# State-space stage of a hybrid backbone block: first weights split earlier, more projections at the opening, transfers by channel block

## The chip, the cores and the metric

The kernel runs on one core of one Trainium2 chip. The metric is the device time of one execution in microseconds (us); lower is better. Engines are named as in the profile: PE (TensorE matmul), PEld (its weight loads), DVE (VectorE), ACT (ScalarE), POOL (GpSimd) and SP (the queue that issues all DMA transfers here). Each engine runs its own instructions in the order in which they stand; semaphores join the engines.

## The reference

One layer over 1024 latent tokens and 256 context tokens of width 1024. The change touches the second of the two token mixers, an S5 state-space model: 512 channels in 32 groups of 16, with 64 complex states a group, run forward and backward.

```python
hl = modulate(rmsnorm(xl, norm1_w[l]), mod_l[0], mod_l[1])
hc = modulate(rmsnorm(xc, norm1_w[l]), mod_c[0], mod_c[1])
pl = jnp.split(hl @ w_in[l], split_idx, axis=-1)
pc = jnp.split(hc @ w_in[l], split_idx, axis=-1)
...
lam_bar, b_bar = s5_discretize(a_re[r], a_im[r], log_step[r], b_re[r], b_im[r])
xs_ctx = s5_scan(flip_if(gc, rev, 1), lam_bar, b_bar, x0)
xs_lat = s5_scan(flip_if(gl, rev, 1), lam_bar, b_bar, xs_ctx[:, -1])
y_lat = y_lat + flip_if(s5_readout(cr, ci, xs_lat), rev, 1)
...
mix_l = (jax.nn.sigmoid(pl[7]) * ya_l + jax.nn.sigmoid(pl[8]) * yb_l) @ w_o[l]
```

`pl[6]` is the S5 input u; `pl[7]` and `pl[8]` are the gates of the merge. The other mixer (gated delta rule) and the MLP with a 3x3 convolution follow and are not touched.

## The kernel before, in words

**Start.** `startup` normalises and transposes the tokens. `modulate` (lines 176 to 200) makes the activations in two parts whose sum is exact enough for float32: ACT rounds a high half (`hl_hi`, `hc_hi`, line 191), DVE recomputes the exact value (line 192), and DVE and POOL by turns subtract to get the low half (`hl_lo`, `hc_lo`, line 194), k block by k block: first latent tokens 0 to 511, then 512 to 1023, then the context.

**The stream of projections.** `gemm_stream` (lines 432 to 478) is a generator. Its 20 jobs are 128 columns of `w_in` each: four for u (units of 512, 512 and 256 tokens), eight for one gate and two for the other (two units of 512), six more with one unit. A job's weights are loaded (`w_raw`, line 442, two buffers), cast to a high half by ACT (`w_hi`, line 447) and subtracted to a low half by POOL (`w_lo`, line 448); the split of the next job's weights and the load of the one after that are issued at the start of a job. Per k block there are three matmuls (high by high, high weights by low activations, low weights by high activations; line 465), and the generator yields after each one:

```python
yield width / 512 * 0.232
```

After a unit, ACT copies it out of PSUM (`gth`, lines 473 and 477) and SP stores it: u to the scratch `u_d` (line 475), gates to `g_d` (line 478).

**The S5 stage.** `s5_stage` works on eight blocks of four groups, h = 0 to 7 ("a group" in the text is one such block of four). For each: `tables` (DVE, lines 484 to 488, products for the g and h tables), `twiddle` (DVE, the same lines on 768 columns), `decays` (ACT), `load` (SP, `s5u` from `u_d`), `weights` (POOL `s5dd`, PE `g_ps`, `ez_ps` and `e_ps`, ACT copies), `toeplitz` (a small DVE sum at line 603, then eight SP copies `s5tm`, line 606), `inputs` (PE `s_ps`, line 618), `rotate` (DVE, lines 629 to 631), `scan` (DVE, lines 637 and 639), `states` (DVE, lines 649 to 652), `outputs` (PE `y_ps`, line 663, ACT Gelu, SP store to `y_d`). Block h+1 is prepared inside block h.

Between these steps `fill(us)` pulls matmuls out of the stream until their booked costs use up the given microseconds, so the order of the program sets how many projection matmuls PE finds between two S5 steps. The whole stage stands under `tc.manual_schedule()`, which keeps each engine's order as written; after it, a scheduler with a model of its own orders instructions. Ahead of the first `fill`, `s5_stage` writes sums for complex products on POOL (`triples`, lines 517 to 523) and three memsets (lines 525 to 527).

Of the kernel before, what the change touches and what calls it, by code (L numbers as in the profile page):

```python
# [61 lines left out]
class Kernel:  # L62
# [188 lines left out]
    def s5_setup(self, sp, tmp):  # L251
        nc, ins, ps = self.nc, self.ins, self.ps
        v = nc.vector
        G = 32
        car = tmp.tile([32, 2, 2, 64], F32, name="car")
        nc.sync.dma_start(car[:, 0], ins["s5_a_re"].rearrange("o r g n -> g (o r) n"))
        nc.sync.dma_start(car[:, 1], ins["s5_a_im"].rearrange("o r g n -> g (o r) n"))
        st = tmp.tile([128, G], F32, name="st")
        for r in range(2):
            nc.sync.dma_start(st[r * 64:(r + 1) * 64, :], ins["s5_log_step"][0, r:r + 1, :].to_broadcast([64, G]))  # L260
        ap = ps.tile([128, 512], F32, tag="dl", name="a_ps")
        for i in range(2):
            self.transpose(ap[:, i * G:(i + 1) * G], car[:, i].rearrange("g r n -> g (r n)"))
        a = tmp.tile([128, 2, G], F32, name="a")
        v.tensor_copy(a, ap[:, :2 * G].rearrange("p (i g) -> p i g", g=G))

# [223 lines left out]
    def s5_stage(self, p, u_d, y_d, stream):  # L490
        nc, ps = self.nc, self.ps
# [9 lines left out]
        def tile(n):  # L501
            return firsts[n].pop() if firsts[n] else new(n)
# [4 lines left out]
        tt = p.tile([128, 2, 768], F32, name="s5tt")  # L507
        tv = tt.rearrange("p c (g m) -> p c g m", g=4)
        t4 = p.tile([128, 4, 768], F32, name="s5t")
        G = 32  # L510
        triples = []
        for name, x, y, n, conj in (("g", self.s5_pg, bb, 8, False), ("h", self.s5_ph, cc, 8, True),
# [12 lines left out]
        g_.memset(b2, 0.0)  # L525
        g_.memset(zo[0:64, :, 0:2], 0.0)
        g_.memset(zo[64:128, :, 768:770], 0.0)
        st = {}
        spent = [0.0]

        def fill(us):
            spent[0] -= us
            while spent[0] < 0:
                c = next(stream, None)
                if c is None:
                    spent[0] = 0.0
                    return
                spent[0] += c

        def gs(h):  # L540
            return slice(4 * h, 4 * h + 4)

        def tables(h):
            hh = p.tile([128, 2, 4, 8, 16], F32, name="s5h", bufs=2)
            gg = p.tile([128, 2, 4, 8, 16], F32, tag="s5r", name="s5g", bufs=2)
            t = [t4[:, i, :512].rearrange("p (g i q) -> p g i q", g=4, i=8) for i in (2, 3)]
            for out, (x, y) in zip((gg, hh), triples):
                xs = [a[:, gs(h), :, None].to_broadcast([128, 4, 8, 16]) for a in x]
                ys = [a[:, gs(h), None, :].to_broadcast([128, 4, 8, 16]) for a in y]
                self.outer3(out[:, 0], out[:, 1], xs, ys, t)  # L550
            st[h] = {"hh": hh, "gg": gg}

        def twiddle(h):
            t3 = tt.rearrange("p c (g a b) -> p c g a b", g=4, a=12)
            t = [t4[:, i].rearrange("p (g a b) -> p g a b", g=4, a=12) for i in (2, 3)]
            xs = [a[:, gs(h), :, None].to_broadcast([128, 4, 12, 16]) for a in triples[2][0]]
            ys = [a[:, gs(h), None, :].to_broadcast([128, 4, 12, 16]) for a in triples[2][1]]
            self.outer3(t3[:, 0], t3[:, 1], xs, ys, t)

        def decays(h):  # L560
            for k in range(4):
                nc.scalar.mul(rho[:, k], self.s5_msk, self.s5_rho[:, 4 * h + k:4 * h + k + 1])

        def load(h):
            u = tile("u")
            r0 = h % 2 * 64
            for j in range(8):
                nc.sync.dma_start(u[j * 16:(j + 1) * 16, :, 0:160],
                                  u_d[h // 2][j, r0:r0 + 64, :].rearrange("(g q) c -> q g c", q=16))
            st[h]["u"] = u  # L570

        def weights(h):
            hh, gg = st[h]["hh"], st[h]["gg"]
            gt = tile("gt")
            dd = p.tile([16, 4, 16], F32, name="s5dd")
            g_.tensor_tensor(dd, self.s5_d[:, gs(h), None].to_broadcast([16, 4, 16]),
                             self.ident[0:16, None, 0:16].to_broadcast([16, 4, 16]), op=OP.mult)
            nc.scalar.copy(b2[0:64, :, :, 0:16], bb[0:64, :, gs(h), :])
            nc.scalar.copy(b2[64:128, :, :, 32:48], bb[64:128, :, gs(h), :])
            for i in range(2):  # L580
                tp = ps.tile([128, 4, 128], F32, tag="tp", name="g_ps")
                for k in range(4):
                    self.transpose(tp[:, k, :], gg[:, i, k].rearrange("p j q -> p (j q)"))
                nc.scalar.copy(gt[:, i], tp)
            e_sb = p.tile([16, 4, 240], F32, tag="s5r", name="s5e", bufs=2)
            ez = ps.tile([128, 4, 16], F32, tag="tp", name="ez_ps")
            for k in range(4):
                for i in range(2):
                    nc.tensor.matmul(ez[0:16, k, :], lhsT=bb[:, i, 4 * h + k, :], rhs=cc[:, i, 4 * h + k, :],
                                     start=(i == 0), stop=(i == 1))  # L590
            fill(1.2)
            ed = ps.tile([128, 4, 128], F32, tag="tp", name="e_ps")
            for k in range(4):
                for i in range(2):
                    nc.tensor.matmul(ed[0:48, k, :], lhsT=b2[:, i, k, :], rhs=hh[:, i, k].rearrange("p i q -> p (i q)"),
                                     start=(i == 0), stop=(i == 1))
            nc.scalar.copy(e_sb[:, :, 0:112], ed[32:48, :, 16:128])
            nc.scalar.copy(e_sb[:, :, 128:240], ed[0:16, :, 0:112])
            st[h].update(gt=gt, e=e_sb, ez=ez, dd=dd)

        def toeplitz(h):
            e_sb = st[h]["e"]
            v.tensor_add(e_sb[:, :, 112:128], st[h]["ez"][0:16], st[h]["dd"])
            tm = tile("tm")
            for j in range(8):
                nc.sync.dma_start(tm[j * 16:(j + 1) * 16], e_sb[:, :, (7 - j) * 16:(7 - j) * 16 + 128])
            st[h]["tm"] = tm
# [15 lines left out]
        def rotate(h):  # L623
            q = t4.rearrange("p c (g m) -> p c g m", g=4)
            for k in range(2):
                ks = slice(2 * k, 2 * k + 2)
                for i in range(2):
                    s = st[h]["s"][2 * k + i][:, None].to_broadcast([128, 2, 2, 192])
                    v.tensor_mul(q[:, 2 * i:2 * i + 2, ks], s, tv[:, :, ks] if i == 0 else tv[:, ::-1, ks])
            v.tensor_sub(t4[:, 0], t4[:, 0], t4[:, 2])  # L630
            v.tensor_add(t4[:, 1], t4[:, 1], t4[:, 3])
# [23 lines left out]
        def outputs(h):  # L655
            s = st.pop(h)
            u, tm, x, hh = s["u"], s["tm"], s["x"], s["hh"]
            yp = ps.tile([128, 4, 128], F32, tag="tp", name="y_ps")
            for k in range(4):
                pairs = ((tm[:, k, :], u[:, k, 32:160]), (hh[:, 0, k].rearrange("p i q -> p (i q)"), x[:, 0, k, :]),  # L660
                         (hh[:, 1, k].rearrange("p i q -> p (i q)"), x[:, 1, k, :]))
                for n, (l, r) in enumerate(pairs):
                    nc.tensor.matmul(yp[:, k, :], lhsT=l, rhs=r, start=(n == 0), stop=(n == 2))
            yo = tile("y")
            nc.scalar.activation(yo, yp, AF.Gelu_apprx_tanh)
            r0 = h % 2 * 64
            for i in range(8):
                nc.sync.dma_start(y_d[h // 2][r0:r0 + 64, i, :].rearrange("(g q) c -> q g c", q=16),
                                  yo[i * 16:(i + 1) * 16])

        fill(14.1)
        tables(0)
        fill(8.0)
        weights(0)
        load(0)
        toeplitz(0)
        twiddle(0)
        decays(0)
        fill(6.0)
        inputs(0)  # L680
        for h in range(8):
            nxt = h + 1 < 8
            rotate(h)
            fill(4.0)
            if h:
                outputs(h - 1)
            if nxt:
                tables(h + 1)
                load(h + 1)
                fill(8.0)  # L690
                weights(h + 1)
            scan(h)
            if nxt:
                toeplitz(h + 1)
            states(h)
            if nxt:
                fill(6.0)
                inputs(h + 1)
                twiddle(h + 1)
                decays(h + 1)  # L700
                fill(3.0)
        fill(1e9)
        outputs(7)

    def late_gates(self, d, g7_d, banks, tags):
# [1012 lines left out]
```

## Time and profile before

| | us |
|---|---|
| median of 3 runs | 1945.08 (1944.63 to 1948.92) |
| profiled execution | 1944.63 |
| its span, first to last instruction | 1942.9 |
| PE busy | 1817.5 (94%) |
| DVE busy | 1342.3 (69%) |
| POOL busy | 818.1 (42%) |
| ACT busy | 722.7 (37%) |
| mean granted PE clock | 0.967 |

The S5 stage with its stream lies between about 63 and 384 us of the span. Busy shares are means over stages with different limits, so for one stage they must be taken from that stage's stretch of the time line. A PE that reads as busy is not always at its peak, since overlapping matmuls are counted whole; the distance between the starts of two matmuls says how fast it goes. The granted clock is 1.0 at 2.4 GHz and 0.5 at 1.2 GHz.

### The profile page before, as it was taken

To read this page: it belongs to the slowest core of one execution; us is meant where nothing else is said; L and a number is where in the kernel's file an instruction comes from. 1 tells how busy PE (TensorE), PEld (TensorE's weight loads), DVE (VectorE), ACT (ScalarE), POOL (GpSimd) and SP (SyncE) were. 2 spreads that over 40 slices of the span, in tenths; PEclk is the share of its full clock that TensorE was granted. 3 is DMA by queue.
4 is the path that set the end of the run, shared out by engine and by line. 5 is a ranking of instruction groups with operands and counts; after the bars stand their busy time and mean duration, and the time that the engine had idled before them with its cause. 6 is when DMAs were issued, how large, how long until landed. Compare 5 with 4: busy or idle time off the path is not lost.

```text
span 1942.9 us, 27849 instructions
## 1 busy us (share of the span) xinstructions
PE 1817.5 (94%) x10922; PEld 1502.9 (77%) x10922; DVE 1342.3 (69%) x1932; ACT 722.7 (37%) x1457; POOL 818.1 (42%) x552
## 2 busy tenths in 40 slices
PE   8289999899999997898899999999999999999997
PEld 3178888777799986787778887788888888888886
DVE  7849999667756546767645334887777777767778
ACT  5513232345444656677642233322212221221222
POOL 1521332346536156545522342444434434442543
PEclk9689999999999998999999999999999999999999
DMA  8033343444412400000344422211111111111102
GB/s 310 24 78 77 90 111 84 130 147 136 136 54 71 129 23 1 2 2 13 125 156 132 129 83 77 65 55 44 44 54 44 54 44 51 47 44 44 55 22 87
DMA packets 190517, 149.30 MB, mean 77 GB/s; under 512 B 25647, under 2 KB 163888, under 8 KB 190386
## 3 DMA queue, kind: packets, MB, share of 16 engines
q1 hardware_dynamic: 190386, 147.52, 25.5%
q8 instruction: 86, 1.41, 0.3%
q14 instruction: 45, 0.37, 0.1%
HBM read 125.99 MB, written 19.40 MB: 75 GB/s over the span
## 4 chain that ended last, share of the span: by engine, by line
PE 58%; DVE 3%; ACT 3%; issue 1%; POOL 1%; DMA 0%; POOLq 0%; SPq 0%; DVEq 0%; ACTq 0%
PE up_ps L227 24%; PE dn_ps L1473 12%; PE pw L227 5%; PE pab L227 4%; PE gl L227 2%; PE pg L227 2%; PE dps L1101 1%; PE ty_ps L1149 1%; PE o_ps L1183 1%; PE ds_ps L1155 1%; PE dps L961 1%; PE ks_ps L1142 1%; ACT Pe L1028 1%; PE pz L227 1%; PE o_ps L1174 1%
## 5 line engine op out<-in xcount | busy, mean ns | idle before, releaser
L1464 DVE SCALAR_TENSOR_TENSOR cacc<-up_ps,colC,cacc 128x945 f32<-128x945 f32 (+3 forms) x360 | 430.3, 1197 | 59.0 <-ACT cacc L1454 51.7
L219 POOL TENSOR_TENSOR w_lo<-w_raw,w_hi 128x1024 fp32r<-128x1024 f32 (+1 forms) x100 | 219.2, 2192 | 417.5 <-ACT w_hi L218 417.1
L227 PE MATMUL up_ps<-h_lo,w_hi 128*128 128x512 f32 x704 | 278.4, 395 | 0.0
L227 PE MATMUL up_ps<-h_hi,w_hi 128*128 128x512 f32 x704 | 277.8, 396 | 0.5 <-DVE cacc L1464 0.5
L227 PE MATMUL up_ps<-h_hi,w_lo 128*128 128x512 f32 x704 | 278.2, 395 | 0.0
L218 ACT CAST w_hi<-w_raw 128x1024 fp32r<-128x1024 f32 (+1 forms) x110 | 105.2, 957 | 371.0 <-PE up_ps L227 163.8
L1483 DVE TENSOR_TENSOR x<-dn_ps,x 128x512 f32<-128x512 f32 x160 | 109.6, 687 | 114.1 <-PE dn_ps L1473 113.0
L227 PEld LDWEIGHTS up_ps<-h_hi,w_hi 128*128 128x128 f32 x704 | 132.3, 188 | 31.9 <-issue 0.9
L227 PEld LDWEIGHTS up_ps<-h_hi,w_lo 128*128 128x128 f32 x704 | 132.6, 188 | 31.0
L227 PEld LDWEIGHTS up_ps<-h_lo,w_hi 128*128 128x128 f32 x704 | 132.5, 188 | 30.9
L448 POOL TENSOR_TENSOR w_lo<-w_raw,w_hi 128x1024 fp32r<-128x1024 f32 x20 | 69.3, 3468 | 195.5 <-ACT w_hi L447 195.4
L465 PE MATMUL pj<-hl_hi,w_lo 128*128 128x512 f32 x272 | 108.7, 400 | 38.4 <-POOL w_lo L448 38.4
L1473 PE MATMUL dn_ps<-wd_lo,g_hi 128*128 128x512 f32 x352 | 138.1, 392 | 0.0
L1473 PE MATMUL dn_ps<-wd_hi,g_lo 128*128 128x512 f32 x352 | 137.5, 391 | 0.0
L1473 PE MATMUL dn_ps<-wd_hi,g_hi 128*128 128x512 f32 x352 | 135.5, 392 | 0.1
L465 PE MATMUL pj<-hl_hi,w_hi 128*128 128x512 f32 x272 | 108.2, 398 | 1.3 <-ACT hl_hi L191 1.3
L465 PE MATMUL pj<-hl_lo,w_hi 128*128 128x512 f32 x272 | 108.7, 400 | 0.8 <-DVE hl_lo L194 0.8
L1287 POOL TENSOR_TENSOR g_lo<-cacc,g_hi 128x1024 fp32r<-128x1024 f32 (+1 forms) x23 | 53.4, 2323 | 92.4 <-ACT g_hi L1286 89.0
L465 PEld LDWEIGHTS pj<-hl_hi,w_lo 128*128 128x128 f32 x272 | 51.8, 190 | 50.2 <-POOL w_lo L448 38.9
L227 PE MATMUL pj<-hl_hi,w_hi 128*128 128x512 f32 (+1 forms) x256 | 90.0, 351 | 0.0
L227 PE MATMUL pj<-hl_hi,w_lo 128*128 128x512 f32 (+1 forms) x256 | 88.9, 347 | 0.0
L227 PE MATMUL pj<-hl_lo,w_hi 128*128 128x512 f32 (+1 forms) x256 | 88.7, 346 | 0.0
(535 smaller groups left out, 4387.3 us busy)
## 6 DMA issues: line engine op xcount, KB each, us to landing
w_raw<-in_w_in SPq DMA_DIRECT2D x46, 512.0 KB, 4.7
w_raw<-in_w_up SPq DMA_DIRECT2D x44, 512.0 KB, 3.8
ada_w<-in_w_ada SPq DMA_DIRECT2D x64, 256.0 KB, 2.7
wd_raw<-in_w_down SPq DMA_DIRECT2D x22, 512.0 KB, 3.6
wa<-in_w_ada SPq DMA_DIRECT2D x16, 512.0 KB, 6.3
g_d<-gth SPq DMA_DIRECT2D x32, 256.0 KB, 2.0
t<-g_d SPq DMA_DIRECT2D x32, 256.0 KB, 3.8
w_raw<-in_w_o SPq DMA_DIRECT2D x16, 512.0 KB, 4.1
```

Source lines behind the costliest of these rows:

```text
L218: self.rounded = nc.scalar.copy(hi[:, :kt, :m], raw[:, :kt, :m]).ins
L219: self.lowered = (eng or nc.gpsimd).tensor_sub(lo[:, :kt, :m], raw[:, :kt, :m], r32(hi[:, :kt, :m])).ins
L227: nc.tensor.matmul(out, lhsT=w[a][:, k, :m], rhs=h[b][k][:, sl] if isinstance(h[b], list) else h[b][:, k, sl], start=(n == 0), stop=(n == ...
L448: nc.gpsimd.tensor_sub(w[1], raw, r32(w[0]))
L465: nc.tensor.matmul(ps[:, :width], lhsT=w[a][:, k], rhs=h[b][:, k, :width], start=(e == 0), stop=(e == 3 * KT - 1))
L961: nc.tensor.matmul(kp[:, h, :], lhsT=self.kT[c][:, h, :], rhs=self.kT[c][:, h, :], start=True, stop=True)
L1028: nc.scalar.copy(pe[g, :, g], pp[g])
L1101: nc.tensor.matmul(o, lhsT=l, rhs=x, start=start, stop=stop, skip_group_check=True)
L1287: (eng or self.nc.gpsimd).tensor_sub(pair[1][sl], x, r32(pair[0][sl]))
L1464: tap[:] = [v.scalar_tensor_tensor(out=o, in0=ui[:, r0 + dy:r1 + dy, c0 + dx:c1 + dx], scalar=cw[:, t * NFT + ct:t * NFT + ct + 1], in1=o, ...
L1473: nc.tensor.matmul(out, lhsT=g[a][:, i * 128:(i + 1) * 128], rhs=w[b][:, h * 512:(h + 1) * 512], start=(first and n == 0), stop=(last and ...
L1483: v.tensor_add(x2, dn, x2)
```

## The change

1. `fill` is defined ahead of the POOL sums, and `fill(0.5)` is called there. The first call of the generator loads and splits the weights of jobs 0 and 1 and issues three matmuls.
2. The opening: 14.1 and 8.0 booked ahead of `weights(0)` become 0.5, 30.0 and 12.0; `twiddle(0)`, `decays(0)` and `load(0)` stand ahead of `weights(0)`, and 6.0 ahead of `inputs(0)` becomes 4.0.
3. In the loop 8.0, 6.0 and 3.0 become 7.0, 5.0 and 2.5. What is left of the stream after block 7 is pulled by `fill(1e9)` as before.
4. `load` and the store in `outputs`: four transfers with all 128 partitions, one for each of the four groups of a block, in place of eight with 16 partitions.

```diff
+        st = {}
+        spent = [0.0]
+
+        def fill(us):
...
+        fill(0.5)
         G = 32
         triples = []
...
             u = tile("u")
             r0 = h % 2 * 64
-            for j in range(8):
-                nc.sync.dma_start(u[j * 16:(j + 1) * 16, :, 0:160],
-                                  u_d[h // 2][j, r0:r0 + 64, :].rearrange("(g q) c -> q g c", q=16))
+            for g in range(4):
+                nc.sync.dma_start(u[:, g, 0:160], u_d[h // 2][:, r0 + 16 * g:r0 + 16 * g + 16, :])
...
-            r0 = h % 2 * 64
-            for i in range(8):
-                nc.sync.dma_start(y_d[h // 2][r0:r0 + 64, i, :].rearrange("(g q) c -> q g c", q=16),
-                                  yo[i * 16:(i + 1) * 16])
-
-        fill(14.1)
+            for g in range(4):
+                r0 = h % 2 * 64 + 16 * g
+                nc.sync.dma_start(y_d[h // 2][r0:r0 + 16].rearrange("q i c -> i q c"), yo[:, g])
+
+        fill(30.0)
         tables(0)
-        fill(8.0)
-        weights(0)
-        load(0)
-        toeplitz(0)
         twiddle(0)
         decays(0)
-        fill(6.0)
+        load(0)
+        fill(12.0)
+        weights(0)
+        toeplitz(0)
+        fill(4.0)
         inputs(0)
...
                 tables(h + 1)
                 load(h + 1)
-                fill(8.0)
+                fill(7.0)
                 weights(h + 1)
...
-                fill(6.0)
+                fill(5.0)
                 inputs(h + 1)
                 twiddle(h + 1)
                 decays(h + 1)
-                fill(3.0)
+                fill(2.5)
```

How the change moves instructions, at three places (rows of the program's order; a name ahead of the arrow is what is written).

POOL from the end of `startup` to the S5 sums, before:

```order
L90 TENSOR_TENSOR rs<-rst,mhalf 128x1
L194 TENSOR_TENSOR hl_lo<-xnT,hl_hi 128x512 x8
L194 TENSOR_TENSOR hc_lo<-xnT,hc_hi 128x256 x4
L521 TENSOR_TENSOR s5dg<-s_pg 128x256
...
L527 MEMSET s5zo 64x2x2
L448 TENSOR_TENSOR w_lo<-w_raw,w_hi 128x1024 x3
```

and with the change:

```order
L90 TENSOR_TENSOR rs<-rst,mhalf 128x1
L448 TENSOR_TENSOR w_lo<-w_raw,w_hi 128x1024 x2
L194 TENSOR_TENSOR hl_lo<-xnT,hl_hi 128x512 x8
L194 TENSOR_TENSOR hc_lo<-xnT,hc_hi 128x256 x4
L534 TENSOR_TENSOR s5dg<-s_pg 128x256
...
L540 MEMSET s5zo 64x2x2
L448 TENSOR_TENSOR w_lo<-w_raw,w_hi 128x1024 x3
```

The low halves of jobs 0 and 1 now stand ahead of the activations' low halves; those of job 2 and later still stand behind the S5 sums.

DVE at the opening, in block 0 (the difference; lines 484 to 488 on 768 columns are `twiddle`, 603 is `toeplitz`, 629 is `rotate`):

```order
 L488 TENSOR_TENSOR s5h<-s5h,s5t 128x512
-L603 TENSOR_TENSOR s5e<-ez_ps,s5dd 16x4x16
 L484 TENSOR_TENSOR s5t<-s_w,s5sw 128x768
...
 L488 TENSOR_TENSOR s5tt<-s5tt,s5t 128x768
+L603 TENSOR_TENSOR s5e<-ez_ps,s5dd 16x4x16
 L629 TENSOR_TENSOR s5t<-s_ps,s5tt 128x2x384 x4
```

The twiddle products no longer stand behind the sum that needs PE's `ez_ps`.

SP around the store of block 5 and the load of block 7, before:

```order
L606 DMA s5tm<-s5e 16x4x128 x8
L478 DMA g_d<-gth 128x512
L442 DMA w_raw<-in_w_in 128x8x128
L478 DMA g_d<-gth 128x512
L668 DMA y_d<-s5y 16x4x128 x8
L568 DMA s5u<-u_d 16x4x160 x8
L478 DMA g_d<-gth 128x512
L442 DMA w_raw<-in_w_in 128x8x128
```

and with the change:

```order
L606 DMA s5tm<-s5e 16x4x128 x8
L478 DMA g_d<-gth 128x512 x2
L442 DMA w_raw<-in_w_in 128x8x128
L668 DMA y_d<-s5y 8x16x128 x4
L569 DMA s5u<-u_d 128x1x160 x4
L478 DMA g_d<-gth 128x512
L442 DMA w_raw<-in_w_in 128x8x128
L606 DMA s5tm<-s5e 16x4x128 x8
```

Two eight-fold issues became four-fold, and one store of a gate moved ahead of the weight load.

## Rows read from the trace of the kernel before

**Rows 1.** Stretches: busy us (count) of PE, PEld, DVE, ACT, POOL; clock, DMA share, GB/s.
```profile
60.00:80.00 20.00, 3.02 (x22) 1.78 (x20) 18.39 (x27) 15.78 (x25) 10.30 (x7) 0.60 0.00 0
80.00:100.00 20.00, 0.00 (x0) 0.00 (x0) 16.58 (x22) 0.00 (x0) 17.04 (x16) 0.50 0.00 0
240.00:260.00 20.00, 20.00 (x118) 16.83 (x117) 19.39 (x20) 6.62 (x15) 9.62 (x3) 1.00 0.46 109
```
**Rows 2.** Time line of the opening: start, duration, engine, line, operation, count, [idle before <-releaser].
```profile
57.52 1.99 ACT L447 CAST w_hi<-w_raw 128x1024 fp32r<-128x1024 f32 x2
63.37 0.55 DVE L192 TENSOR_SCALAR xnT<-xnT,am,modc 128x512 f32<-128x512 f32 x1 [0.88 <-ACT hl_hi L191]
65.23 1.45 POOL L194 TENSOR_TENSOR hl_lo<-xnT,hl_hi 128x512 fp32r<-128x512 f32 x1 [8.71 <-DVE xnT L192]
...
88.02 0.41 DVE L194 TENSOR_TENSOR hc_lo<-xnT,hc_hi 128x256 fp32r<-128x256 f32 x1
101.12 5.50 POOL L448 TENSOR_TENSOR w_lo<-w_raw,w_hi 128x1024 fp32r<-128x1024 f32 x2
103.90 0.79 PE L465 MATMUL pj<-hl_hi,w_lo 128*128 128x512 f32 x1 [38.41 <-POOL w_lo L448]
119.74 0.37 ACT L473 COPY gth<-pj 128x256 f32<-128x256 f32 x1 [2.33 <-PE pj L465]
```
**Rows 3.** Time line of PE: projection matmuls, and s_ps of two following groups.
```profile
108.33 0.48 PE L465 MATMUL pj<-hl_hi,w_hi 128*128 128x512 f32 x1
109.58 0.40 PE L465 MATMUL pj<-hl_hi,w_lo 128*128 128x512 f32 x1
115.72 0.39 PE L465 MATMUL pj<-hl_hi,w_lo 128*128 128x512 f32 x1
...
225.81 2.77 PE L618 MATMUL s_ps<-s5u,s5gt 128*128 128x192 f32 x16
256.67 2.77 PE L618 MATMUL s_ps<-s5u,s5gt 128*128 128x192 f32 x16
```
**Rows 4.** Time line of DVE in the groups, and of GpSimd's weight subtractions.
```profile
133.29 0.94 DVE L488 TENSOR_TENSOR s5tt<-s5tt,s5t 128x768 f32<-128x768 f32 x1
138.61 2.36 POOL L448 TENSOR_TENSOR w_lo<-w_raw,w_hi 128x1024 fp32r<-128x1024 f32 x1 [14.84 <-ACT w_hi L447]
139.74 3.55 DVE L629 TENSOR_TENSOR s5t<-s_ps,s5tt 128x768 f32<-128x768 f32 x4 [5.51 <-PE s_ps L618]
207.29 0.69 DVE L486 TENSOR_TENSOR s5h<-s5dh,s_c 128x512 f32<-128x512 f32 x1 [0.43 <-PE y_ps L663]
226.66 3.55 DVE L629 TENSOR_TENSOR s5t<-s_ps,s5tt 128x768 f32<-128x768 f32 x4 [0.52 <-PE s_ps L618]
238.15 0.69 DVE L486 TENSOR_TENSOR s5h<-s5dh,s_c 128x512 f32<-128x512 f32 x1 [1.73 <-PE y_ps L663]
240.25 3.58 POOL L448 TENSOR_TENSOR w_lo<-w_raw,w_hi 128x1024 fp32r<-128x1024 f32 x1 [11.88 <-ACT w_hi L447]
241.65 3.73 DVE L639 TENSOR_TENSOR_SCAN s5zo<-s5rho,s5t 64x736 f32<-64x736 f32 x1
247.11 1.69 DVE L639 TENSOR_TENSOR_SCAN s5zo<-s5rho,s5t 64x736 f32<-64x736 f32 x1
```
**Rows 5.** Time line of PE and DVE in the last group.
```profile
346.18 3.65 PE L595 MATMUL e_ps<-s5h,s5b 128*48 128x128 f32 x16 [5.03 <-ACT s5gt L584]
357.14 3.55 DVE L629 TENSOR_TENSOR s5t<-s_ps,s5tt 128x768 f32<-128x768 f32 x4 [0.71 <-PE s_ps L618]
380.79 1.09 PE L663 MATMUL y_ps<-s5x,s5h 128*128 128x128 f32 x4 [0.59 <-DVE s5x L651]
```
**Rows 6.** Time line of the SP queue, and the cast that waited for a weight load.
```profile
331.10 3.60 SPq L668 DMA_DIRECT2D y_d<-s5y  x8
334.80 3.65 SPq L568 DMA_DIRECT2D s5u<-u_d  x8
343.97 1.04 ACT L447 CAST w_hi<-w_raw 128x1024 fp32r<-128x1024 f32 x1 [6.91 <-DMA w_raw<-in_w_in]
```

More of the change, by code (lines that the diff above doesn't have):

```diff
@@ L509, in s5_stage @@
         t4 = p.tile([128, 4, 768], F32, name="s5t")
+        st = {}
+        spent = [0.0]
+        def fill(us):
+            spent[0] -= us
+            while spent[0] < 0:
+                c = next(stream, None)
+                if c is None:
+                    spent[0] = 0.0
+                    return
+                spent[0] += c
+        fill(0.5)
         G = 32
@@ L527, in s5_stage @@
         g_.memset(zo[64:128, :, 768:770], 0.0)
[L528 to L538, printed above, removed]
         def gs(h):
```

## The prediction

> **What bounds the kernel now.** Read the granted clock and the chain first: one core, and the chain that ended last is mostly TensorE from the query projections on. The change sits earlier, in the state-space (S5) stage, so the question is what ends last there and whether a gain in it is carried to the end. The table by stretches comes next [rows 1]: from 60 to 100 us TensorE has 3 us of work in 40, while VectorE is busy for 35 of them and GpSimd for 27; by 240 to 260 us TensorE is full and VectorE has 19.4 of 20. So there are two regimes: an opening in which TensorE starves, and a steady stage in which TensorE and VectorE are nearly balanced.
>
> The time line of the opening tells why it starves [rows 2]. The two high halves of the first projection weights are cast on ScalarE at 57.5. The first matmul that needs a low half waits 38.41 us, until 103.90, for GpSimd's subtraction at line 448, which starts only at 101.12 although GpSimd had idled 8.71 us ahead of 65.23: it is written behind the low halves of the activations and the S5 sums. The first projection's last copy-out starts at 119.74.
>
> In the steady stage one group of S5 lasts 30.86 us by its s_ps starts [rows 3]. A full-rate 512-column matmul starts every (115.72 - 109.58) / 27 = 0.2274 us [rows 3], where the code books 0.232, so booked time counts 0.98. The group's bookings, 4 + 8 + 1.2 + 6 + 3 = 22.2, are 21.8 us; the remaining 9.0 are S5's own matmuls. VectorE needs three group starts from 139.74 to 226.66, 86.92 us, less the two waits shown, 0.43 and 0.52 [rows 4]: 28.66 a group of its own work. That is with about one operation a group held up: the scan at 241.65 takes 3.73 beside a GpSimd weight subtraction, its twin at 247.11 takes 1.69.
>
> **The change, part by part.** *Weights first.* The pair of low halves now precedes the activations' low halves on GpSimd, where the time line has a gap. TensorE then takes the first projection at the pace at which activations appear; the last one on VectorE ends at 88.43 [rows 2], and the last three half-width matmuls put its end at about 89.2, against 119.7. The risk is that the pair, from 58.5 (first cast done) for two times 2.36 [rows 4], ends near 63.4, just where VectorE starts the activations at 63.37 [rows 2]. I take 0.5 us of delay for all that follows; the bounds are 0 and the 2.0 that the held-up scan lost. So 89.7.
>
> The rule that speaks against this edit: the Trainium skill, SBUF — State Buffer, section Who interferes with whom, says that VectorE in a two-port mode, or with two SBUF inputs, and GpSimd hold a shared port pair in turns, for a whole instruction each. The scan's row agrees. By it the first VectorE operation would wait for the rest of the second subtraction, some 0.5 us, and the sum is the same.
>
> The second projection needs 60 times 0.2274 = 13.6 us, so TensorE reaches the third at 103.3. Its low half is still behind the S5 sums on GpSimd: 101.12 + 0.5, and 2.75 for one of the two that took 5.50 [rows 2], is 104.4. TensorE stands 1.1 us.
>
> *Longer opening.* Before, from the first projection's end to the first rotation is 139.74 - 119.74 = 20.0 us [rows 2, 4]. The bookings ahead of that rotation rise from 14.1 + 8 + 1.2 + 6 = 29.3 to 0.5 + 30 + 12 + 1.2 + 4 = 47.7, which is 18.0 us more at 0.98. First rotation: 89.7 + 1.1 + 20.0 + 18.0 = 128.8, only 10.9 earlier although TensorE is 29 ahead: the opening spends the rest on projections, which later groups then need not carry. The twiddle and decay steps, moved ahead of the Toeplitz step, fill a time in which VectorE has nothing else and cost nothing; were that cover gone, the twiddle step's five operations of 0.94 [rows 4] would cost 4.7 us.
>
> *Smaller fills.* A group now books 4 + 7 + 1.2 + 5 + 2.5 = 19.7, so TensorE needs 19.3 + 9.0 = 28.3, below VectorE's 28.66. VectorE becomes the bound. Its wait for the output matmuls, 1.73 at 238.15 [rows 4], shrinks to 1.2 since 0.5 is booked less ahead of them; once VectorE trails by that much it is gone, so I count it once. Last rotation: 128.8 + 1.2 + 7 times 28.66 = 330.6, against 357.14 [rows 5]. From there to the last output matmul 23.65 [rows 5]: 354.2, against 380.79, which is **26.5 earlier**.
>
> TensorE itself is done sooner: 864 full-width matmuls are 196.5 us, 27.3 of them done at 104.4; 169.2 and at most 8 times 9.0 more end at 343 to 346. So it stands some 8 to 10 us ahead of the last outputs and restarts at the lower of its two clocks. At 103.90, after its long wait, 11 matmuls took 4.43 us instead of 2.5 [rows 3]: 1.9 lost. After the stop at 346.18, 5.03 us long, the e_ps batch shows the same slowness [rows 5]. I subtract 1.9.
>
> *Transfers with all partitions.* Each group's u load and y store becomes four issues instead of eight. The eight stores hold the SP queue 3.60 us and the eight loads 3.65 [rows 6], 0.45 each; behind them in that queue came the weight load for which ScalarE's cast at 343.97 had waited 6.91 [rows 6], and that stopped TensorE for 5.03 at 346.18 [rows 5]. Half of that queue time, 3.6 us a group, goes. The order also puts the last half-width weights' load ahead of that group's store. The one stop of 5 us should vanish, but it lies inside the TensorE time that no longer decides; in the last VectorE period it is already left out of 28.66. Gain counted: 0; bounds 0 and 1.8 (the last store's four issues, ahead of the next stage's weight loads). The data itself must be in place 20 us later, so a slower landing of these transfers costs nothing unless that cover goes.
>
> Behind the stage the scheduler places some 100 matmuls of the delta rule in slightly other gaps; no row prices that, and I allow 3 us either way. Nothing later waits on a fixed time, so the gain is carried.
>
> Sum: 26.5 - 1.9 = 24.6. The profiled execution lasted 1944.63 (span 1942.9 and 1.7 around it), the median is 0.45 higher; **1944.63 - 24.6 = 1920.0**.
>
> **The rivals.** *TensorE stays the bound.* If GpSimd, with 1.8 instead of 2 weight subtractions a group, holds VectorE up less, the groups take TensorE's 28.3 and a shorter tail; the outputs cannot start before 343 to 346. For: the scan alone loses 2.0 in a group. Against: the late half-width projections bring subtractions twice as often. Gain 35 to 37 without the restart: 1908 to 1910.
>
> *The SP queue takes over.* The Toeplitz copies (eight issues) wait in order for VectorE's small addition; with VectorE trailing, weight loads and stores behind them slip, and the groups stay at 30.86. Then 128.8 + 7 times 30.86 + 23.65 = 368.5, a gain of 12.3: 1932. For it: the queue is where the stop at 346.18 came from. Against: half the issues are gone.
>
> *Slower.* The same stop, 5.03 of waiting and 1.7 or so of slow clock, in each of the seven groups: ScalarE's cast, waiting for a weight load, sits ahead of the g_ps copies. Then 28.66 + 6.7 a group is 128.8 + 247.5 + 23.65 = 400, 19 later: 1964. It decides from 3.8 us a group on (26.5 / 7). Against: a full-width projection gives a load 11 us, and the stop occurred once.
>
> *It does not do what it says.* If the weights were not what the opening waits for, the time stays at 1945. Against: GpSimd's gap and the cast at 57.5 are in the rows.
>
> **How the numbers follow.** Forecast 0.65 (1914 to 1926 with the bounds of the opening's delay, the store, the later order, and 28.3 to 29.2 a group), TensorE bound 0.13, SP queue 0.12, slower 0.06, no effect 0.04. The range 1910 to 1932 holds the forecast and about the inner half of two rivals. About 0.2%, 4 us, can be told from no change; the first three cases are all faster by more: faster 0.90, within 0.2% 0.04, slower 0.06.
>
> **What would show it.** Right: TensorE working from 63 to 89 us, first gth copies well before 90; the first rotation near 129 and later ones 28.3 to 29.2 apart; TensorE idle for several us ahead of the last y_ps, released by the last state sums near 354; u and y issues at half their number. Wrong: rotations 31 apart (SP), cast waits for weight loads in most groups (slower), no idle ahead of the last y_ps (TensorE bound), or a delta stage whose length moves by more than 3 us.

## The result, and the profile after

| | before | after |
|---|---|---|
| median, us | 1944.86 (1944.4 to 1948.92) | 1924.01 (1923.37 to 1924.65) |
| profiled execution | 1944.63 | 1924.12 |
| its span | 1942.9 | 1922.4 |
| mean granted PE clock | 0.967 | 0.973 |

The ratio is 0.9888, 95% interval 0.9871 to 0.9905. The forecast was 1920.0 with a range of 1910 to 1932. The profiled executions differ by 20.5 us where the sum said 24.6.

The table by stretches after the change, with the columns of [rows 1]:

```profile
60.00:80.00 20.00, 14.99 (x53) 9.19 (x53) 18.48 (x25) 16.08 (x26) 13.20 (x8) 0.74 0.10 27
80.00:100.00 20.00, 17.77 (x80) 13.07 (x79) 16.50 (x23) 2.49 (x4) 16.59 (x15) 1.00 0.30 73
...
340.00:360.00 20.00, 13.24 (x60) 11.55 (x59) 15.67 (x13) 3.94 (x6) 7.43 (x9) 0.77 0.38 113
```

From 60 to 100 us TensorE now works 32.8 us where it worked 3.0. The third line is the price at the other end: TensorE is busy for 13.2 of the last 20 us of the stage, and the granted clock falls to a mean of 0.77.

The time line of the opening, which answers to [rows 2]:

```profile
58.45 4.95 POOL L448 TENSOR_TENSOR w_lo<-w_raw,w_hi 128x1024 fp32r<-128x1024 f32 x2 [2.11 <-ACT w_hi L447]
62.30 1.13 DVE L171 SCALAR_TENSOR_TENSOR am<-modc,colA 128x16 f32<-128x16 f32 x1
64.31 0.55 DVE L192 TENSOR_SCALAR xnT<-xnT,am,modc 128x512 f32<-128x512 f32 x1 [0.88 <-ACT hl_hi L191]
89.16 0.41 DVE L194 TENSOR_TENSOR hc_lo<-xnT,hc_hi 128x256 fp32r<-128x256 f32 x1
90.81 0.37 ACT L473 COPY gth<-pj 128x256 f32<-128x256 f32 x1 [4.83 <-PE pj L465]
102.46 2.78 POOL L448 TENSOR_TENSOR w_lo<-w_raw,w_hi 128x1024 fp32r<-128x1024 f32 x1
```

The pair of low halves is subtracted at 58.45, 43 us earlier, and the first projection's last copy stands at 90.81 instead of 119.74. The small `am` operation, on which all activations depend, takes 1.13 us while the second subtraction runs.

The groups, on VectorE (a `rotate` begins each group) and GpSimd:

```profile
130.10 3.55 DVE L629 TENSOR_TENSOR s5t<-s_ps,s5tt 128x768 f32<-128x768 f32 x4 [6.83 <-PE s_ps L618]
223.64 2.77 DVE L484 TENSOR_TENSOR s5t<-s_ph,s5sh 128x512 f32<-128x512 f32 x1
242.89 0.94 DVE L488 TENSOR_TENSOR s5tt<-s5tt,s5t 128x768 f32<-128x768 f32 x1
243.93 3.55 DVE L629 TENSOR_TENSOR s5t<-s_ps,s5tt 128x768 f32<-128x768 f32 x4
301.48 3.55 DVE L629 TENSOR_TENSOR s5t<-s_ps,s5tt 128x768 f32<-128x768 f32 x4
332.50 3.55 DVE L629 TENSOR_TENSOR s5t<-s_ps,s5tt 128x768 f32<-128x768 f32 x4
...
223.45 2.42 POOL L448 TENSOR_TENSOR w_lo<-w_raw,w_hi 128x1024 fp32r<-128x1024 f32 x1 [6.09 <-ACT w_hi L447]
238.20 7.90 POOL L448 TENSOR_TENSOR w_lo<-w_raw,w_hi 128x1024 fp32r<-128x1024 f32 x1 [11.64 <-ACT w_hi L447]
```

Six groups from 130.10 to 301.48 are 28.56 us each, against TensorE's 30.86 before [rows 3]; after the first one no rotation waits for `s_ps` any more, and VectorE has no other wait in the groups, so VectorE is the bound. The last distance is 31.02.

The end of the stage on TensorE, and SP's issues there, which answer to [rows 5, 6]:

```profile
334.35 0.50 PE L465 MATMUL pj<-hl_hi,w_hi 128*128 128x512 f32 x1 [2.11 <-ACT w_hi L447]
355.21 1.40 PE L663 MATMUL y_ps<-s5x,s5h 128*128 128x128 f32 x4 [6.76 <-DVE s5x L651]
359.39 1.06 PE L663 MATMUL y_ps<-s5x,s5h 128*128 128x128 f32 x4
360.10 0.77 PE L745 MATMUL pj<-hl_hi,wb 128*48 128x512 f32 x1
...
307.68 2.57 SPq L668 DMA_DIRECT2D y_d<-s5y  x4
310.36 2.53 SPq L569 DMA_DIRECT2D s5u<-u_d  x4
313.48 0.39 SPq L442 DMA_DIRECT2D w_raw<-in_w_in  x1
```

TensorE stands 6.76 us ahead of the last outputs, and these then take 4.9 us where they took 2.9 before. Four issues hold SP 2.5 us, 0.64 each; eight had held it 3.6, 0.45 each. The two stretches of the last outputs, with the columns of [rows 1], after and before:

```profile
355.21:360.10 4.89, 4.88 (x22) 4.79 (x23) 0.55 (x1) 0.00 (x0) 0.28 (x6) 0.50 0.00 0
...
380.79:383.64 2.85, 2.74 (x22) 2.54 (x23) 0.54 (x1) 0.57 (x2) 2.70 (x6) 1.00 0.54 182
```

The granted clock is 0.50, that is 1.2 GHz, after the stop of 6.76 us, and 1.00 before, where TensorE had stood 0.59 us [rows 5].

Where the gain stands along the way, from the starts of the same instructions in both traces (pg is the last gate projection ahead of the delta rule, ty_ps the last batch of a product in the delta rule's recurrence, dn_ps the last of the MLP):

| | before | after | earlier by |
|---|---|---|---|
| first rotation | 139.74 | 130.10 | 9.6 |
| last rotation | 357.14 | 332.50 | 24.6 |
| first of the last y_ps batches | 380.79 | 355.21 | 25.6 |
| first matmul of the next stage | 383.64 | 360.10 | 23.5 |
| last pg | 695.12 | 673.06 | 22.1 |
| last ty_ps | 941.91 | 922.03 | 19.9 |
| last dn_ps | 1931.31 | 1910.77 | 20.5 |

So 25.6 us are won inside the stage, 2.0 are given back at once at the slow clock, and another 3.0 behind the stage.

### The profile page after: what moved, and what is told of

The parts are those of the page before. It is cut to its first block, busy times and chain, and to the rows that moved or that the text cites. A ratio compares the mean times of both kernels' runs of the same rounds, so it can differ in the third digit from the quotient of the medians.

```text
span 1922.4 us, 27770 instructions
## 1 busy us (share of the span) xinstructions
PE 1825.2 (95%) x10922; PEld 1505.4 (78%) x10922; DVE 1344.2 (70%) x1932; ACT 723.4 (38%) x1457; POOL 815.2 (42%) x552
## 4 chain that ended last, share of the span: by engine, by line
PE 59%; DVE 4%; ACT 3%; issue 1%; POOL 1%; DMA 0%; POOLq 0%; SPq 0%; DVEq 0%; ACTq 0%
PE up_ps L227 25%; PE dn_ps L1472 12%; PE pw L227 5%; PE pab L227 4%; PE gl L227 2%; PE pg L227 2%; PE dps L1100 1%; PE ty_ps L1148 1%; PE dps L960 1%; PE o_ps L1173 1%; PE o_ps L1182 1%; PE ds_ps L1154 1%; PE pz L227 1%; PE ks_ps L1141 1%; ACT Pe L1027 1%
## 5 line engine op out<-in xcount | busy, mean ns | idle before, releaser
L448 POOL TENSOR_TENSOR w_lo<-w_raw,w_hi 128x1024 fp32r<-128x1024 f32 x20 | 65.4, 3273 | 172.5 <-ACT w_hi L447 161.2
L1516 ACT ACTIVATE cacc<-cacc 128x1024 f32<-128x1024 f32 x22 | 23.3, 1058 | 175.7 <-DVE cacc L1463 175.7
```

The costliest lines, as they stand in the source:

```text
L448: nc.gpsimd.tensor_sub(w[1], raw, r32(w[0]))
L1516: nc.scalar.activation(ga, ga, AF.Silu)
```

## The experiments

| | us | ratio to before, 95% | first rotation | last y_ps ends | delta stage |
|---|---|---|---|---|---|
| before | 1944.86 | | 139.7 | 383.9 | 246.8 |
| the change | 1924.01 | 0.9888 (0.9871 to 0.9905) | 130.1 | 360.5 | 249.0 |
| w_first_only | 1923.26 | 0.989 (0.9871 to 0.9908) | 117.9 | 362.2 | 247.3 |
| opening_only | 1948.33 | 1.0018 (1.0008 to 1.0027) | 157.1 | 388.2 | 248.9 |
| old_transfers | 1924.15 | 0.9893 (0.9878 to 0.9908) | 130.4 | 360.4 | 248.6 |
| opening_22 | 1913.0 | 0.9836 (0.982 to 0.9853) | 122.3 | 351.3 | 248.7 |
| transfers_only | 1929.51 | 0.9909 (0.9894 to 0.9924) | 140.0 | 383.8 | 235.3 |
| split_pieces | 1920.24 | 0.9861 (0.9846 to 0.9875) | 129.6 | 357.6 | 248.2 |
| split_dve | 1912.74 | 0.9823 (0.9807 to 0.9839) | 121.1 | 351.7 | 246.7 |
| opening_16 | 1911.72 | 0.9817 (0.9801 to 0.9834) | 116.4 | 350.6 | 248.1 |
| transfers_same_order | 1944.24 | 0.9992 (0.9981 to 1.0002) | 140.6 | 384.8 | 246.0 |
| opening_19 | 1890.47 | 0.9715 (0.9695 to 0.9734) | 119.1 | 348.1 | 226.0 |
| opening_16_order4 | 1904.05 | 0.9772 (0.9753 to 0.9791) | 116.5 | 353.3 | 236.2 |
| opening_19_old_transfers | 1890.14 | 0.9704 (0.9685 to 0.9722) | 119.2 | 348.3 | 225.3 |

Times are medians; each ratio is against runs of before on the same chip (1944.96, 1947.15, 1945.86 and 1948.34 in the four sets). The last three columns are read from each trace; the delta stage is counted from the start of the last pg to the start of the last batch of ty_ps.

### Which part carries the gain

**w_first_only**: the kernel before with one edit.

```diff
         t4 = p.tile([128, 4, 768], F32, name="s5t")
+        st = {}
+        spent = [0.0]
+
+        def fill(us):
...
+        fill(0.5)
```

> Only the first two weight splits are written early; opening bookings (14.1, 8, 6), loop bookings (8, 6, 3), step order and eight-fold transfers as before. Theory A (TensorE's empty opening is the whole gain, the rest only moves it about): TensorE has the first projection at 90, the bookings ahead of the first rotation put it at 112 to 116, groups stay TensorE-bound at 30.9 us, so last rotation 328 to 332, last y_ps 352 to 356, time 1920 to 1926, within 4 us of the change. Theory B (the longer opening and smaller fills are needed to turn the early start into time): groups longer than 30.9 because stops like the 5.03 us one come back, last y_ps beyond 360, time 1930 or more.

1923.26, as theory A had it: the whole gain, with the old bookings and transfers. In detail the run was later than expected, with the first rotation at 117.9, the last at 335.8 and the last y_ps at 361, which is beyond the 360 that theory B named: the stop of 5.0 us for the cast stayed in the last group, and TensorE stood 3.8 us once for `s5dd`. Two things bring it to the change's time. TensorE waits only 0.72 us for the last outputs (359.09) and takes them at the full clock, so a start that is 3.9 us later than in the change becomes a next stage that is 1.9 us later (361.95 and 360.10). And the delta stage is 1.7 us shorter. Counted at the end of the last y_ps, this one edit brings 21.7 of the change's 23.4 us.

**opening_only**: the change without the early call and with the old transfers.

```diff
-        fill(0.5)
         G = 32
```

> Only the opening (30, 12, 4 and the step order) and the smaller loop fills (7, 5, 2.5); the weight splits stay behind the sums, transfers eight-fold as before. Theory A: first projection done at 119.7 as before, first rotation 139.7 + 17.5 = 157, groups 28.6 us (VectorE bound), last rotation 358 to 360, last y_ps 380 to 383 against 380.8: time 1943 to 1949, no gain, perhaps 2 us lost. Theory B: the smaller fills carry a part of the gain of their own: 1930 to 1938.

1948.33, 0.18% slower, as theory A had it, though the last y_ps ends at 388.2 and not at 380 to 383. The groups are 28.6 apart as in the change (157.14 to 328.94 for six), but they begin 17.4 later, and TensorE stands 7.0 us ahead of the last outputs. The longer opening and the smaller fills are worth nothing by themselves; they only choose on which side of the groups the projections are done.

**old_transfers**: the change, with the eight-fold load and store of the kernel before.

```diff
-            for g in range(4):
-                nc.sync.dma_start(u[:, g, 0:160], u_d[h // 2][:, r0 + 16 * g:r0 + 16 * g + 16, :])
+            for j in range(8):
+                nc.sync.dma_start(u[j * 16:(j + 1) * 16, :, 0:160],
+                                  u_d[h // 2][j, r0:r0 + 64, :].rearrange("(g q) c -> q g c", q=16))
...
```

> The change with eight-fold transfers of 16 partitions put back for s5u and y_d. Theory A: transfers are off the path; 1922 to 1926, rotations within 0.3 us a group of the change. Theory C (the SP queue, freed by the four-fold transfers, is a part of the gain): the weight loads slip behind 2 us more of issues a group, casts wait, 1928 or more.

1924.15, with each rotation 0.3 us later and the same distances. The transfers are off the path.

### How far the opening should go

**opening_22** and **opening_16**: the change with 22 or 16 in one place.

```diff
-        fill(30.0)
+        fill(22.0)
```

> The change with 22 instead of 30 us booked ahead of the first tables step. Theory A (VectorE's eight groups and tail, from the first rotation on, set the end, and TensorE has 7 us to spare behind its last projection): first rotation 8 us earlier at 122, groups still 28.6, last rotation about 325, last y_ps about 347, no idle and no clock restart: 8 to 10 us faster than the change, 1914 to 1916. Rival D (TensorE's total work ends at 343 to 346 plus stops and becomes the bound again): last y_ps 350 to 352, 1918 to 1921.

1913.0, a little better than theory A's 1914, but with the last y_ps where rival D put it: it ends at 351.3, and theory A had 347. The groups' first and last rotation, and TensorE at the end:

```profile
122.32 3.55 DVE L629 TENSOR_TENSOR s5t<-s_ps,s5tt 128x768 f32<-128x768 f32 x4 [8.33 <-PE s_ps L618]
322.09 3.55 DVE L629 TENSOR_TENSOR s5t<-s_ps,s5tt 128x768 f32<-128x768 f32 x4
...
348.21 0.40 PE L465 MATMUL pj<-hl_hi,w_lo 128*128 128x512 f32 x1
348.44 0.39 PE L663 MATMUL y_ps<-s5u,s5tm 128*128 128x128 f32 x2
348.66 0.61 PE L663 MATMUL y_ps<-s5x,s5h 128*128 128x128 f32 x4
...
351.04 0.47 PE L745 MATMUL pj<-hl_hi,wb 128*48 128x512 f32 x1
```

Projections run up to 348.21 and the outputs follow without a gap, at a granted clock of 1.00: from the first product with `s5x` to the next stage 2.4 us where the change needs 4.9. The next stage starts 9.1 us earlier than with the change. So VectorE's sums are in time, and TensorE's own work ends last.

> The change with 16 instead of 30 us ahead of the first tables step. Theory D (at 22 TensorE and VectorE are balanced, so TensorE's total work is the bound below): first rotation at 116 to 117, but later groups or the tail wait for TensorE, last y_ps ends at 349 to 352 as with 22, 1912 to 1914. Theory A alone (VectorE's chain still sets the end): last y_ps 6 us earlier than with 22, 1907.

1911.72: VectorE's chain starts 5.9 us earlier still, and the last y_ps ends only 0.7 earlier. TensorE is the bound again, as theory D had it. What it still loses are short stops: 2.34 us for a low half at 324.26 with 22, and 1.12 (318.09), 0.93 and 0.59 with 16.

### The subtractions on GpSimd

**split_pieces**: each subtraction of line 448 in four.

```diff
-            nc.gpsimd.tensor_sub(w[1], raw, r32(w[0]))
+            for k in range(0, KT, 2):
+                nc.gpsimd.tensor_sub(w[1][:, k:k + 2], raw[:, k:k + 2], r32(w[0])[:, k:k + 2])
```

> The change with every weight subtraction on GpSimd cut into four of a quarter of the columns. Theory A (VectorE is the bound and one of its operations in a group is held up for the length of a GpSimd subtraction): groups shrink from 28.6 towards 27.8, the held-up scan and sums of the last group lose 0.6 each instead of 2 to 3, last y_ps at 347 to 351, time 1917 to 1921, and the am operation at 62.3 loses 0.5 or less instead of 0.96. Rival E (the pieces hold up as much in sum, or TensorE is the bound): groups 28.4 to 28.8, 1922 to 1926.

The time, 1920.24, is theory A's, but its mechanism fell for the groups: six from 129.61 to 300.64 are 28.5 each, as rival E had it. VectorE and GpSimd in one group:

```profile
222.57 0.68 DVE L489 TENSOR_TENSOR s5g<-s5g,s5t 128x512 f32<-128x512 f32 x1
223.29 1.11 DVE L485 TENSOR_TENSOR s5t<-s_ph,s5sh 128x512 f32<-128x512 f32 x1
224.32 1.22 DVE L486 TENSOR_TENSOR s5t<-s_ph,s_c 128x512 f32<-128x512 f32 x1
225.47 1.22 DVE L487 TENSOR_TENSOR s5h<-s5dh,s_c 128x512 f32<-128x512 f32 x1
226.61 1.22 DVE L488 TENSOR_TENSOR s5h<-s5t 128x512 f32<-128x512 f32 x1
227.75 0.78 DVE L489 TENSOR_TENSOR s5h<-s5h,s5t 128x512 f32<-128x512 f32 x1
...
222.96 4.33 POOL L449 TENSOR_TENSOR w_lo<-w_raw,w_hi 128x256 fp32r<-128x256 f32 x4 [5.52 <-ACT w_hi L447]
```

Five operations of 0.68 lose 2.15 us together; in the change one lost 2.09 (2.77 at 223.64) and the next 0.1. Beside these products the pieces spread the loss and do not lessen it. Beside the scans four pieces cost 1.64 us (four scans from 141.08) where one subtraction had cost 2.18 (141.57 in the change), but twice they end so late that VectorE waits 1.51 us for the sum `s5dd` behind them on GpSimd:

```profile
178.43 0.21 DVE L604 TENSOR_TENSOR s5e<-ez_ps,s5dd 16x64 f32<-16x64 f32 x1 [1.51 <-POOL s5dd L577]
346.84 2.28 DVE L740 TENSOR_TENSOR wb<-wb_raw,wb 128x128 fp32r<-128x128 f32 x1
```

The gain is in the last group, which takes 20.36 us instead of 22.71 from its rotation until the sums `s5x` let TensorE go (352.46 instead of 355.21), and it is hardly by the pieces. In the change two subtractions of the next stage's weights, which are not cut, hold VectorE up there by 2.09 and 2.16 us (343.93 and 351.12); here only one does, by 2.0 (346.84, an operation of 0.28 otherwise). The pieces themselves save 0.1. And `am` took 0.17 again, but the first activation's two operations took 0.67 and 1.10 (0.55 and 0.69 unhindered): the first projection's copy stands 28.33 us behind `modc` (90.98 and 62.65), against 28.74 in the change (90.81 and 62.07).

**split_dve**: opening_22, with job 0's subtraction on VectorE.

```diff
-        ready = split(raws.pop(0))
+        ready = split(raws.pop(0), nc.vector)
```

> 22 us ahead of the first tables step, and the first of the two early weight splits on VectorE, in its gap of 1.25 us at 59.1; the second stays on GpSimd, alone. Theory A (the pair on GpSimd holds up VectorE at 62.3 and with it all activations by 1.0 us, and TensorE, balanced with VectorE, passes it on): am at 62.3 takes 0.2, first activation at 63.4, everything to the end 0.8 to 1.2 earlier than with opening_22: 1911.8 to 1912.3. Rival F (the activations' pace is set elsewhere, or the split delays the last transposes by as much): no difference from 1913.

```profile
59.10 1.21 DVE L448 TENSOR_TENSOR w_lo<-w_raw,w_hi 128x1024 fp32r<-128x1024 f32 x1
...
62.60 0.17 DVE L171 SCALAR_TENSOR_TENSOR am<-modc,colA 128x16 f32<-128x16 f32 x1
63.66 0.55 DVE L192 TENSOR_SCALAR xnT<-xnT,am,modc 128x512 f32<-128x512 f32 x1 [0.89 <-ACT hl_hi L191]
...
90.14 0.37 ACT L473 COPY gth<-pj 128x256 f32<-128x256 f32 x1 [4.82 <-PE pj L465]
```

The first half held: the pair on GpSimd costs the opening 1.2 us (copy at 90.14 instead of 91.36, rotations at 121.11 instead of 122.32). The second half fell: the last y_ps start at 351.04 instead of 350.67, and 1912.74 cannot be told from 1913.0. TensorE loses the 1.2 us, and 0.4 more, between 324 and 327. In both runs it stands 2.3 us for a late low half (2.34 at 324.26 in opening_22, 2.32 at 323.03 here); in opening_22 it goes on at the full clock, here the clock falls:

```profile
324.26:327.12 2.86, 2.86 (x13) 2.36 (x14) 2.69 (x5) 1.53 (x2) 0.41 (x1) 1.00 0.83 192
...
324.26:327.25 2.99, 2.99 (x8) 2.32 (x7) 2.99 (x4) 2.94 (x4) 2.10 (x1) 0.50 0.77 210
```

So rival F has the time, but not by its reasons: the opening did pass on its 1.2 us, and a clock of 0.50 for 3 us took them back.

### The transfers alone, and what they set off

**transfers_only**: the kernel before with the change's `load` and store, the reverse of the diff of old_transfers.

> The kernel before with the four-fold transfers of s5u and y_d alone. Theory A (transfers off the path): 1942 to 1947. But TensorE is the bound in the groups here, so the one stop of 5.03 us in the last group, which comes from a weight load late in the SP queue, is on the path: if the queue time saved is what made it, it shrinks by up to 3.6 us and the time falls to 1940 to 1942 (theory C); if the load is late for another reason (it waits for its buffer, or stands behind the s5tm copies that wait for VectorE), the stop stays at 4 to 5 us and the time at 1944 to 1946.

1929.51, which none of the theories had: 17.6 us in the medians and 12.6 in the traces, although the stage itself gains nothing (last y_ps ends at 383.8 against 383.9; the stop for the cast is 4.2 us instead of 5.0). Of the 12.6, 11.5 arise between 695 and 942 us, in the delta rule, where no transfer of S5 is left. The same stretch, from the last pg to the last ty_ps, in the kernel before:

```profile
695.10:941.90 246.80, 210.18 (x2679) 183.83 (x2678) 158.97 (x359) 172.68 (x486) 140.90 (x141) 0.92 0.04 13
```

and in transfers_only:

```profile
695.00:930.30 235.30, 208.66 (x2662) 182.62 (x2662) 149.94 (x357) 170.26 (x484) 139.67 (x140) 0.91 0.03 10
```

The instructions are the same to within the window's ends, and they are packed tighter. VectorE's busy time falls too, by 9.0 us: most of it is 64 copies (`Rf` and `Qf`) that take 23.9 us together instead of 29.7. And TensorE's second largest wait of before between 640 and 950 us is gone (in total, times, longest, in us):

```profile
PE o_ps L1174 <- DVE o L1190: 4.8, 2, 4.5
```

The two programs differ there: the scheduler that orders everything behind S5 starts from its own model of S5, and the other transfers shift that model. In the traces TensorE's 3,642 matmuls from the first pz to the first gl are the same in both, but their order differs in 97 places. **transfers_same_order** was made to tell order from transfers.

It is transfers_only with one number changed:

```diff
-        fill(14.1)
+        fill(13.0)
```

> The kernel before with the four-fold transfers, as in transfers_only, and 13.0 instead of 14.1 us booked at the opening; with this number the scheduler places the delta stage behind S5 exactly as in the kernel before, on all engines, which it did not in transfers_only. Theory G (the 13 us of transfers_only are the delta stage's other order, 235 instead of 247 us from the last pg matmul to the last ty_ps; the transfers themselves are worth nothing): delta stage 246 to 248, last y_ps 382 to 384, time 1943 to 1947. Theory C (the transfers themselves bring it, by whatever they leave undisturbed later): 1930 to 1933.

1944.24, delta stage:

```profile
696.90:943.00 246.10, 211.24 (x2680) 184.82 (x2679) 158.98 (x359) 172.98 (x486) 141.08 (x141) 0.92 0.04 13
```

Theory G holds: with the order of before (all but 6 of the 3,642 matmuls stand at the same place), the new transfers are worth nothing. Two more orders were run behind the better openings: **opening_19**,

```diff
-        fill(30.0)
+        fill(19.0)
```

> The change with 19 instead of 30 us ahead of the first tables step; between opening_16 and opening_22 for the S5 stage, but with a third order of the delta stage behind it. S5 by theory D: last y_ps at 350 to 351, as with 16 and 22. If the delta stage's order is worth what transfers_only suggests, its length from the last pg matmul to the last ty_ps is anywhere from 235 to 250 and the time is 1912 plus its difference from 248; if the length does not depend on the order, 248 and 1911 to 1913.

and **opening_16_order4**:

```diff
-        fill(30.0)
+        fill(16.0)
...
-        fill(12.0)
+        fill(12.5)
```

> The change with 16 and 12.5 us booked at the opening, and a fourth order of the delta stage, the one furthest from the order before. S5: last y_ps at 350 to 351. Delta stage as in opening_19: 235 to 250 us if the order decides, 248 if not; time 1912 plus the difference from 248.

1890.47 and 1904.05, with delta stages of 226.0 and 236.2. The first is shorter than the 235 to 250 that the expectation allowed, and the last y_ps, expected at 350 to 351 in both, ends at 348.1 and 353.3. The stretch in opening_19:

```profile
661.30:887.30 226.00, 200.62 (x2662) 176.36 (x2661) 148.99 (x357) 169.09 (x483) 137.79 (x137) 0.94 0.03 10
```

TensorE's wait for VectorE's `o`, 4.8 us before and with the change, is gone here as in transfers_only and opening_16_order4, and it stands in transfers_same_order and opening_16: it goes with the long orders. That it is what makes them long is not shown; it is a part of the difference at most. The S5 stage is like opening_22's, with the last y_ps 3.2 us earlier, mostly since the stop of 2.34 us is missing; 23 of the 33.5 us to the change come from the delta stage.

**opening_19_old_transfers** is opening_19 with the diff of old_transfers.

> opening_19 with the eight-fold transfers put back; TensorE's delta stage has the same order as in opening_19. Theory G (the length of the delta stage follows its order, the transfers are worth nothing): delta stage 225 to 228 us, time 1889 to 1894. Theory C (the four-fold transfers have a part in it): 1900 or more.

1890.14, delta stage 225.3: the same order gives the same length with other transfers. This is the best version found, with opening_19: 55 to 58 us faster than the runs of before beside them.

## Why the prediction was right, point by point

- **Weights first.** Right, and the whole of the gain (w_first_only). I took 0.5 us for the delay of the activations; it is 0.9 (first activation at 64.31 against 63.37 [rows 2]), and 1.1 at their end (89.16 against 88.02). The rule of the Trainium skill, SBUF — State Buffer, section Who interferes with whom, that of a VectorE operation with two SBUF inputs and a GpSimd one that reads SBUF the second blocks until the first is done, had named the right place. The trace agrees: `am` takes 1.13 us and ends with the second subtraction (63.43 and 63.40), and it takes 0.17 without. The end of the first projection was put at 89.7; its copy starts at 90.81.
- **The third job's stop.** Put at 1.1 us from a late subtraction; TensorE waited 0.3 for it. The subtraction began at 102.46, worked out as 101.6, and took 2.78, but TensorE came later too.
- **Longer opening.** First rotation forecast 128.8, measured 130.10.
- **VectorE becomes the bound.** Right: 28.56 a group where I had 28.66. The one wait of 1.2 for the output matmuls never came, and the last distance was 2.4 us longer than 28.66: three operations are held up there by 2.2, 1.9 and 0.3 us (2.89 at 311.41, 2.56 at 322.48, 1.22 at 305.07), since the half-width projections bring subtractions twice as often, which I had used only as an argument against a rival. Last rotation forecast 330.6, measured 332.50.
- **The tail.** 23.65 taken from before; 22.71 measured. Start of the last outputs forecast 354.2, measured 355.21. What neither the prediction nor its row says: 6.8 us of the 22.71 are four operations of VectorE held up beside GpSimd subtractions (6.2 in the tail of before), 4.2 of it by two for the next stage's weights:

```profile
343.93 3.77 DVE L637 TENSOR_TENSOR_SCAN s5zo<-s5rho,s5t 64x736 f32<-64x736 f32 x1
351.12 2.83 DVE L649 TENSOR_TENSOR s5t<-s5tt,s5zo 128x512 f32<-128x512 f32 x1
...
343.77 2.38 POOL L219 TENSOR_TENSOR w_lo<-w_raw,w_hi 128x1024 fp32r<-128x1024 f32 x1 [1.42 <-ACT w_hi L218]
350.98 2.42 POOL L219 TENSOR_TENSOR w_lo<-w_raw,w_hi 128x1024 fp32r<-128x1024 f32 x1 [4.83 <-ACT w_hi L218]
```

- **The restart.** 1.9 subtracted; 2.0 lost (25.58 to 23.54 us). The row had been misread: from 103.90 to 108.33 there are 10 matmuls and not 11, so 4.43 us stand against 2.3, and the loss there was 2.2. TensorE's own work ended at 348.5 and not at 343 to 346, so it stood 6.76 us and not 8 to 10.
- **Transfers.** Counted 0, and old_transfers and transfers_same_order show 0. The queue time saved is 2.15 us a group (7.25 to 5.10), not the 3.6 of the text, since each larger transfer takes 0.64 to issue. The one stop of 5.0 did not vanish; it is 2.1 at 334.35.
- **Behind the stage.** "I allow 3 us either way" is the weakest step, an allowance with nothing under it. The 3.0 lost there makes up most of the 4.1 between forecast and result, just inside it; but over the kernels run here the delta stage is 225 to 249 us long, and its length goes with its order. That the change's order is within 2.2 us of the order before was luck that the prediction did not know it needed. With a delta stage of 226.0 instead of 249.0 the same change would have come out at 1901, by this difference alone, which is below the range.

Of the rivals, "TensorE stays the bound" is refuted by its 6.76 us of idle time, "the SP queue takes over" by groups of 28.56 and by old_transfers, "slower" by a single cast stop of 2.1 us, and "no effect" by the opening. A rival was missing: another order behind the stage, for which the prediction had only its allowance.

The sizes add up: 25.58 us at the first of the last y_ps batches, less 2.04 at the restart, less 1.48 up to the last pg, less 2.18 in the delta stage, plus 0.66 in the rest, is 20.54. What the change left lying was 11 us: it books 30 us at the opening, where 22 lets VectorE start 8 us sooner and TensorE fill the last group instead of standing.

## What to carry to other kernels

Where one engine starves at the start of a stage, look for the instruction it waits for and for what is merely written ahead of it; that one move was worth all of this change. How much work to do ahead of a chain on another engine is then a balance: stop when both end together, since idle time at the end costs twice, once as waiting and once in the clock. And where a scheduler orders a later stage, compare that stage's length and order before crediting an edit: a neutral edit here moved the time by 13 us in the traces, and with the best order found that stage is 23 us shorter than with the change.

## What the runs showed of the hardware that was not expected

- A GpSimd subtraction beside VectorE's run of operations on two SBUF operands can be the one that waits. At 238.20 in the change it takes 7.90 us, and at 207.34 one takes 10.01, where the free ones take 2.36 [rows 4]. The first of them ends at 246.10, so its own 2.36 would begin at 243.74, just as the last of the twiddle products ends (242.89 and 0.94), ahead of the rotation that reads PSUM. VectorE lost nothing there. Another, at 223.45, went at once and cost VectorE 2.09. What decides who goes first was not settled.
- Cutting such a subtraction into four hardly cheapens it: 2.15 us lost over five products instead of 2.19 over two, and 1.64 over four scans instead of 2.18 in one.
- The four-fold stores take SP 0.64 us each to issue (2.57 for four), the eight-fold ones 0.45 (3.60 for eight [rows 6]). It is not the 128 partitions alone: a weight load with as many takes 0.39 (313.48).
- After 6.76 us of standing, TensorE's output step ran at a granted clock of 0.50 and took 4.9 us instead of the 2.4 at 1.00 without the stop (opening_22), and the first two starts of the next stage were 0.58 us apart instead of 0.31.
- A stop of the same length can leave the clock or bring it down: after 2.34 us (opening_22) and 2.11 us (the change, 334.35) the granted clock stayed at 1.00, after 2.32 us (split_dve) it fell to 0.50 within 1.2 us of the restart, for some 3 us. What decides it was not settled.
